# Split weights placed 64 bytes off, or level with, the other operand of their matmuls

## Chip, cores and metric

The kernel runs on one core of one Trainium2 chip. The metric is the device time of one execution in microseconds; the median of three runs of the kernel before is 2693.97 us. All engine names are those of the profile: PE (TensorE), PEld (its weight loads), DVE, ACT, POOL, SP.

## What is computed

The reference runs a two-layer network on one sequence of 512 tokens with a width of 1024, and a further layer behind it, all in float32. Cut to what matters:

```
for layer in range(2):
    h = h + 0.5 * rms_norm(swiglu(rms_norm(h, g[0]), ffn_w_in, ffn_w_out), g[1])
    u = rms_norm(h, g[2])
    m = rwkv7_time_mix(u, ...) if layer == 0 else swa_sinks(u, k_sh, v_sh, ...)
    h = h + rms_norm(m, g[3])
    h = h + 0.5 * rms_norm(swiglu(rms_norm(h, g[4]), ffn_w_in, ffn_w_out), g[5])
x = second_block(h, ...)   # adaptive norm, w_in, two attentions, two branches, w_out, final norm
```

Most of the work is dense products: four feed-forward blocks (1024 to 2 x 2816 and back to 1024), the r, k, v and output projections of the time mix, the projections of the attention, and those of the second block.

## The kernel before

**Products.** A float32 weight is used as two float32r numbers, a high and a low part. `weights` (L146) loads 128 x 1024 weights (512 KB) with a DMA on SP into `wr`, writes the high half of a tile `whl` [128, 2, 1024] on ACT (L153) and the low half on DVE (L154). `mmhl` (L161) issues three products for each 128 x 128 block, L164, L165 and L166: high x high, high x low, low x high. Each has a weight load of its own, and the weight load of the next product runs beside the current product. The moving operand has 512 columns (the whole sequence) or 256 (a half of it). Halves are used where the second half of the sequence is not ready yet, or where the first half has to be done early.

**Feed-forward blocks 0, 2 and 3** (`ffn`, L313; the right-hand pools `a`, `sg`, `wx` are opened there). For hidden columns f = 0, 1, 2 the two halves of the sequence are multiplied one after the other with 256 columns (`gu<-xn`, weights of f = 2 in the pool `wx`). For the other f the products have 512 columns. The way back (`dtile`, L383, tile `o<-a`) comes in two parts: fh = 0 with 512 columns for all 8 output blocks d; fh = 1 with 512 columns for d = 0 and 1, and with 256 columns, first half then second half, for d = 2 to 7. `piece(i)` (L378) makes the weight tiles of that part: 11 pieces of 8 blocks, block b = 11 d + i; pieces 7 to 10 of fh = 1 lie in `wx`.

**Feed-forward block 1** (class `Halves`, L411) works with 256 columns throughout. `xA` (first half) lies in the pool `xnp`, `xB` (second half) in `xb`. `hidden` (L417) takes xA alone for f = 0 to 13, xB alone for f = 11 to 13 and 0 to 10, and both in turn for f = 14 to 21. Its hidden values lie in `xnp` (named `pair`), in `mp` or in the block's own right-hand pool (both named `a`); `out` (L436) multiplies them.

**Time mix** (`dense`, L571; `run`, L813). The first half's `r` projection uses mixed inputs `mx` with float32r weights; the other products of this stage are plain float32 (`mxe` with `wraw`, L592). The chunked recurrence (`Core`) runs beside the second half's projections. `out_half` (L963) is the output projection, with `y` in `xnp` for the first half and in `yb` for the second.

**Attention and second block.** `attention` (L1294) projects q (`psq`), k (`psk`, from `kvn`) and v (`psv`) and multiplies by the output weights (`o<-ohl`). `second` (L1614) multiplies by `w_in2` (`ps<-xn`, `psg<-xn`), by `w_uq` and `w_ukv` (`cqh`, `ckvh`), by the branch weights (`ps<-br`) and by `w_out2` (`o<-mg`). Every third tile of the gates' weights lies in the pool `wsx`, the others in `whl`.

**Memory.** Pools are stacks. One grows from the low addresses of a partition (`left`), the other down from byte 229344 (`right`). Tiles start at multiples of 32 bytes. In the program of before, the start addresses of the operands of these products, modulo 128, are:

```
left   xnp 32   hp 32   mp 32   whl 32   wraw 32   mx 32
right  a 96   wx 96   xb 96   yb 96   lat (cqh, ckvh) 96   lcst (wq) 96   wsx 96   fin (br) 96
right  ato (kvn, ohl) 0
```

The offsets inside the tiles (a block of 512 bytes, the low half 4096 bytes on, a half of the sequence 1024 bytes on) are multiples of 128, so a pool has one remainder. `const` (8096 bytes at byte 1152) lies under the whole left stack. A new tile whose place was held by an older one waits for the last use of that one.

**Order of work.** The instructions of an engine run in the order in which the program gives them; SP issues its transfers in order. Waits come from the tiles alone.

Of the kernel before, what the change touches and what calls it, by code (L numbers as in the profile page):

```python
# [8 lines left out]
F32 = mybir.dt.float32  # L9
# [8 lines left out]
P = 128  # L18
# [2 lines left out]
FT = 22  # L21
FH = 11
HALVES = ((0, 256), (256, 256))
FULL = ((0, 512),)


# [59 lines left out]
class Net:  # L86
    def __init__(self, tc, ctx, ins, outs):
        self.tc, self.nc, self.ctx = tc, tc.nc, ctx
        self.ins, self.outs = ins, outs
        nc = tc.nc  # L90
        self.const = self.pool("const", 1)
        self.tail = iter(())
        self.dead = None
        self.open_x()
        self.open_mm()
        self.ones = self.const.tile([P, P], F32, name="ones")
        nc.vector.memset(self.ones, 1.0)
        self.ident = self.const.tile([P, P], F32, name="ident")
        nc.gpsimd.affine_select(out=self.ident, in_=self.ones, pattern=[[1, P]], compare_op=ALU.is_equal, fill=0.0, base=0, channel_multiplier=-1)
        nv = ins["vecs"].shape[1]  # L100
        self.vecs = self.const.tile([P, nv], F32, name="vecs")
        nc.scalar.dma_start(out=self.vecs, in_=ins["vecs"])
        self.eps = self.const.tile([P, 1], F32, name="eps")
        nc.vector.memset(self.eps, 1e-6)
        self.bk = self.const.tile([P, 2], F32, name="bk")
        nc.scalar.dma_start(out=self.bk, in_=ins["b_k"])
        self.rows = self.const.tile([P, 272], F32, name="rows")
        nc.scalar.dma_start(out=self.rows, in_=ins["rows"])

        self.rx = self.const.tile([P, T], F32, name="rx")  # L110
        self.halfg = self.const.tile([P, 96], F32, name="halfg")
        nc.vector.tensor_scalar(out=self.halfg, in0=self.vecs[:, 0:96], scalar1=0.5, scalar2=None, op0=ALU.mult)
# [30 lines left out]
            self.small = self.pool("small", 2, self.wctx)  # L143


    def weights(self, src, pool=None, cols=1024, hl=None):  # L146

        nc = self.nc
        if hl is None:
            hl = (pool or self.whl).tile([P, 2, 1024], F32R, tag="whl", name="whl")  # L150
        raw = self.wraw.tile([P, 1024], F32, tag="wraw", name="wr")
        nc.sync.dma_start(out=raw[:, :cols], in_=src)
        nc.scalar.activation(out=hl[:, 0, :cols], in_=raw[:, :cols], func=AF.Copy)  # L153
        nc.vector.tensor_tensor(out=hl[:, 1, :cols], in0=raw[:, :cols], in1=hl[:, 0, :cols].bitcast(F32), op=ALU.subtract)  # L154
        return hl
# [157 lines left out]
    def ffn(self, idx, gpost, after_half, side=(), early=()):  # L313
        nc = self.nc
        win, wout = self.ins["ffn_w_in"][idx], self.ins["ffn_w_out"][idx]
        with ExitStack() as es:
            ap = self.pool("a", 12, es, side="right")
            tp = self.sg = self.pool("sg", 2, es, side="right")
            wx = self.pool("wx", 4, es, side="right")
            nsp = 3  # L320
            for fh in range(2):
# [15 lines left out]
                for t0, n in HALVES if first else ():  # L337
                    for f in first:
                        if t0 == 0:
                            a[f] = ap.tile([P, 2, T], F32R, tag="a", name="a")  # L340
                            w[f] = [self.weights(win[2 * f + j], wx if f == 2 else None) for j in range(2)] if f or not early else early
                        ps[f] = self.mm.tile([P, 2, n], F32, tag="mm", name="gu")
                        if t0 == 0:
                            for j in range(2):
                                for k in range(KT):
                                    self.mm3(ps[f][:, j], w[f][j], k, self.xn[k], t0, n, k == 0 and j == 0, k == KT - 1, skip_group_check=True)
                            run(islice(self.tail, 4))
                    if t0:
                        for fl in (first[:2], first[2:]):
                            for k in range(KT):  # L350
                                for f in fl:
                                    for j in range(2):
                                        self.mm3(ps[f][:, j], w[f][j], k, self.xn[k], t0, n, k == 0 and j == 0, k == KT - 1, skip_group_check=True)
                    else:
                        run(self.tail)
                    for f in first:
                        act(f, ps[f][:, 0], ps[f][:, 1], t0, n)
# [19 lines left out]

                def piece(i):  # L378
                    if i not in pcs:
                        pcs[i] = self.weights(wout[fh * 11 + i], wx if fh == 1 and i >= 7 else None)  # L380
                    return pcs[i]

                def dtile(d, t0, n):  # L383
# [27 lines left out]
class Halves:  # L411
# [5 lines left out]
    def hidden(self, f, halves, w=None):  # L417

        N, nc = self.N, self.N.nc
        w = w or [N.weights(self.win[2 * f + j]) for j in range(2)]  # L420
        ps = [N.mm.tile([P, 2, 256], F32, tag="mm", name="gu") for _ in halves]
        for j in range(2):
            for k in range(KT):
                for (x, a, hf), p in zip(halves, ps):
                    N.mm3(p[:, j], w[j], k, x[k], 0, 256, j == 0 and k == 0, k == KT - 1, skip_group_check=True)
                yield
        for (x, a, hf), p in zip(halves, ps):
            r = N.rx[:, 256 * hf:256 * hf + 256]
            s = N.small.tile([P, 2, 256], F32, tag="gu", name="gu", bufs=1)
            nc.vector.tensor_tensor(out=s, in0=p, in1=r[:, None, :].to_broadcast([P, 2, 256]), op=ALU.mult)  # L430
            nc.scalar.activation(out=s[:, 0], in_=s[:, 0], func=AF.Silu)
            nc.vector.tensor_tensor(out=s[:, 0], in0=s[:, 0], in1=s[:, 1], op=ALU.mult)
            nc.scalar.activation(out=a[0], in_=s[:, 0], func=AF.Copy)
            nc.vector.tensor_tensor(out=a[1], in0=s[:, 0], in1=a[0].bitcast(F32), op=ALU.subtract)

    def out(self, fh, halves):  # L436

        N = self.N
        for d in range(KT):
            ps = N.mm.tile([P, 2, 256], F32, tag="mm", name="o")  # L440
            for i in range(FH):
                b = d * FH + i
                if b % 8 == 0:
                    w = N.weights(self.wout[fh * FH + b // 8])
                for j, (a, _) in enumerate(halves):
                    hi, lo = a[fh * FH + i]
                    N.mmhl(ps[:, j], w, b % 8, hi, lo, i == 0 and j == 0, i == FH - 1, skip_group_check=True)
                yield
            for j, (_, sink) in enumerate(halves):
                sink(d, ps[:, j])  # L450
# [62 lines left out]
class Rwkv:  # L513
# [57 lines left out]
    def dense(self, hf, tmp, exact, mx, mxe):  # L571
# [10 lines left out]

        def weights(src, ex):
            if not ex:
                return N.weights(src)
            w = N.wraw.tile([P, 1024], F32, tag="wraw", name="wraw")
            nc.sync.dma_start(out=w, in_=src)
            return w
# [224 lines left out]
    def run(self, h_spill, gpost, gpre, ffn, gffn, after_half):  # L813
# [9 lines left out]
        e1 = ExitStack()  # L823
        tmp = N.pool("tmp1", 1, e1)
        with ExitStack() as e2:
            mx, mxe = N.pool("mx", 12, e2), N.pool("mxe", 16, e2)
            first = self.dense(0, tmp, (0,), (12, lambda: mx.tile([P, 2, 256], F32R, tag="mx", name="mx")), (16, lambda: mxe.tile([P, 256], F32, tag="mxe", name="mxe")))

            run(islice(first, 8))
# [133 lines left out]
    def out_half(self, hf, y, m, h_spill, gpost, after):  # L963
# [3 lines left out]
        nc.sync.dma_start(out=N.h[:, :, t0:t0 + n], in_=h_spill.rearrange("(k p) t -> p k t", p=P)[:, :, t0:t0 + n])  # L967
        acc = N.small.tile([P, n], F32, tag="acc", name="acc")
        for d in range(KT):
            w = N.weights(N.ins["w_rkvo"][3, d])  # L970
            ps = N.mm.tile([P, T], F32, tag="mm", name="o")
            for k in range(KT):
                N.mm3(ps[:, :n], w, k, y[k], 0, n, k == 0, k == KT - 1)
# [320 lines left out]
def attention(N, kvd, rd, gpost, after_half):  # L1294

    nc = N.nc
    W = 128
    with ExitStack() as es:
        one = N.pool("at1", 1, es, side="right")
        qp = N.pool("atq", 2, es, side="right")  # L1300

        oh = N.pool("ato", 8, es, side="right")
        with ExitStack() as e2:
            N.mm, N.st, scp = Turns(N.ma), None, Turns(N.mb, N.mb, N.ms, N.mb, N.ms)
            vec = lambda n: N.vecs[:, 8 * VEC[n]:8 * VEC[n] + 8]
# [20 lines left out]

            early = []
            for t in range(2):
                w = N.weights(N.ins["w_qo"][0, t])
                early.append((w, N.mm.tile([P, T], F32, tag="mm", name="psq")))  # L1330
                for k in range(KT):
                    N.mm3(early[t][1][:, 0:256], w, k, N.xn[k], 0, 256, k == 0, k == KT - 1, skip_group_check=True)
# [2 lines left out]
            for a in range(2):  # L1335
# [2 lines left out]
                for k in range(KT):  # L1338
                    N.mm3(pk[a], w, k, kvn[k], 0, T, k == 0, k == KT - 1)
                run(islice(N.tail, 3))  # L1340
            w = [N.weights(N.ins["w_kv"][2 + j]) for j in range(2)]
            pv = [scp.tile([P, 2, 256], F32, tag="sc", name="psv") for _ in range(2)]
            for k in range(KT):
                j, q = k // 4, slice(256 * (k % 4), 256 * (k % 4) + 256)
# [116 lines left out]
            def out(d, ks, pool=None, t0=0, n=T):  # L1461

                if d not in wo:
                    wo[d] = N.weights(N.ins["w_qo"][1, d])
                if ks[0] == 0:
                    po_[d] = pool.tile([P, T], F32, tag="sc" if pool is scp else "mm", name="o")
                for k in ks:
# [146 lines left out]
def second(N, out, angd, hs):  # L1614
# [61 lines left out]
    with ExitStack() as e1:  # L1676
# [2 lines left out]

        early = []  # L1680
        for i in range(5):
            w, ps = N.weights(N.ins["w_in2"][i]), N.mm.tile([P, T], F32, tag="mm", name="ps")
            for k in range(KT):
                N.mm3(ps[:, 0:256], w, k, N.xn[k], 0, 256, k == 0, k == KT - 1, skip_group_check=True)
            early.append((w, ps))
# [302 lines left out]

    def dtile(d, t0, n):
        if d not in ws:  # L1990
            ws[d] = N.weights(N.ins["w_out2"][d])
        ps = N.mm.tile([P, T], F32, tag="mm", name="o")
        for k in range(KT):
            N.mm3(ps[:, :n], ws[d], k, mg[k], t0, n, k == 0, k == KT - 1)
# [19 lines left out]
def net(tc, ins, out):  # L2014
    with ExitStack() as ctx:
# [8 lines left out]
        N.open_w()  # L2024
        early = []
        for hf in range(2):
            early.append(N.weights(ins["ffn_w_in"][0, hf]))
            N.load_h(ins["xT"], hf)

        def to_products(gcol):  # L2030
# [46 lines left out]
```

## Time and profile before

| | |
|---|---|
| median of 3 runs | 2693.97 us (2688.26 to 2700.58) |
| profiled execution | 2691.58 us |
| its span on the core | 2689.8 us |
| PE, PEld busy | 2613.0 us (97%), 2269.7 us (84%) |
| DVE, ACT, POOL busy | 1477.3 (55%), 1189.4 (44%), 110.5 (4%) |
| mean granted TensorE clock | 0.987 of full speed |
| DMA over the span | 344.21 MB, mean 128 GB/s |

The sum of the prediction is made against the profiled execution; the difference between its time and its span (1.8 us) is what lies around the span. A busy PE is not a PE at its peak: a product is shown with the time that it takes from end to end, and products overlap. The pace of a stream is the distance from one start to the next.

### The profile page before, as it was taken

The page shows a single profiled execution, that of the slowest core. Times are in us where ns is not written, and L with a number is a line of the kernel's source. Part 1 is how long each engine was busy: PE and PEld are TensorE (multiplying, and loading weights), DVE is VectorE, ACT ScalarE, POOL GpSimd, SP SyncE. Part 2 cuts the span into 40 slices and gives each one's busy share as a digit, 9 for nine tenths or more (in the row PEclk, how much of TensorE's full clock was granted, in tenths as well). Part 3 has the DMA queues.
Part 4 walks back from the last instruction along what each step waited for, and adds up shares of the span by engine and source line. Part 5 has one row for each costly group of instructions (what it writes and reads, how often), then busy time and mean ns, then how long its engine had stood idle before and what let it go on. Part 6 is the DMA issues. An engine that isn't in the chain of part 4 may idle for free.

```text
span 2689.8 us, 44078 instructions
## 1 busy us (share of the span) xinstructions
PE 2613.0 (97%) x17458; PEld 2269.7 (84%) x17458; DVE 1477.3 (55%) x3065; ACT 1189.4 (44%) x2156; POOL 110.5 (4%) x140
## 2 busy tenths in 40 slices
PE   8999998899999999999999999999999999999998
PEld 7888897778789999999988889779888898877777
DVE  7734456565647556448652446647424456334655
ACT  5232337555455555345532334556322334445643
POOL 0000000000000000000000000330000000000310
PEclk9999999999999999999999999999999999999999
DMA  6632316774675464235443233112322333213352
GB/s 208 210 111 97 103 62 213 228 205 133 195 226 152 126 214 131 95 111 186 129 148 99 94 118 122 64 40 88 102 94 95 102 103 118 83 45 92 121 166 91
DMA packets 207557, 344.21 MB, mean 128 GB/s; under 512 B 66164, under 2 KB 136180, under 8 KB 207352
## 3 DMA queue, kind: packets, MB, share of 16 engines
q1 hardware_dynamic: 206920, 341.13, 40.1%
q8 instruction: 137, 2.24, 0.3%
q14 instruction: 68, 0.56, 0.1%
q10 hardware_dynamic: 432, 0.28, 0.0%
HBM read 298.51 MB, written 41.26 MB: 126 GB/s over the span
## 4 chain that ended last, share of the span: by engine, by line
PE 86%; DMA 5%; DVE 4%; ACT 2%; issue 1%; SPq 0%; DVEq 0%; ACTq 0%
PE gu L165 11%; PE gu L164 11%; PE gu L166 11%; PE o L164 8%; PE o L166 8%; PE o L165 7%; PE ps L592 3%; PE ps L164 2%; PE ps L165 2%; PE ps L166 2%; PE psg L164 2%; PE psg L165 2%; PE psg L166 2%; PE z L1788 1%; PE st L175 1%
## 5 line engine op out<-in xcount | busy, mean ns | idle before, releaser
L153 ACT ACTIVATE whl<-wr 128x1024 fp32r<-128x1024 f32 x417 | 438.8, 1058 | 722.2 <-PE gu L166 391.8
L154 DVE TENSOR_TENSOR whl<-wr,whl 128x1024 fp32r<-128x1024 f32 x417 | 508.9, 1225 | 378.2 <-ACT whl L153 377.1
L164 PE MATMUL gu<-xn,whl 128*128 128x512 f32 (+1 forms) x1200 | 435.5, 365 | 9.0 <-ACT xn L242 6.9
L165 PE MATMUL gu<-xn,whl 128*128 128x512 f32 (+1 forms) x1200 | 437.7, 366 | 2.2 <-DVE xn L243 2.0
L166 PE MATMUL gu<-xn,whl 128*128 128x512 f32 (+1 forms) x1200 | 436.7, 365 | 0.8 <-DVE whl L154 0.8
L166 PE MATMUL o<-a,whl 128*128 128x256 f32 (+1 forms) x950 | 302.8, 320 | 0.0
L165 PE MATMUL o<-a,whl 128*128 128x256 f32 (+1 forms) x950 | 302.7, 320 | 0.0
L164 PE MATMUL o<-a,whl 128*128 128x256 f32 (+1 forms) x950 | 301.5, 320 | 0.0
L164 PEld LDWEIGHTS gu<-xn,whl 128*128 128x128 f32 x1200 | 226.1, 189 | 45.0 <-ACT xn L242 7.1
L165 PEld LDWEIGHTS gu<-xn,whl 128*128 128x128 f32 x1200 | 226.9, 189 | 39.4 <-DVE xn L243 3.5
L166 PEld LDWEIGHTS gu<-xn,whl 128*128 128x128 f32 x1200 | 227.1, 189 | 37.3 <-DVE whl L154 1.2
L165 PE MATMUL gu<-pair,whl 128*128 128x256 f32 x704 | 199.4, 284 | 1.1 <-DVE pair L243 1.1
L166 PE MATMUL gu<-pair,whl 128*128 128x256 f32 x704 | 198.2, 282 | 1.2 <-DVE whl L154 1.2
L164 PE MATMUL gu<-pair,whl 128*128 128x256 f32 x704 | 198.8, 284 | 0.0
L166 PEld LDWEIGHTS o<-a,whl 128*128 128x128 f32 x950 | 178.9, 188 | 15.4
L165 PEld LDWEIGHTS o<-a,whl 128*128 128x128 f32 x950 | 178.9, 188 | 15.2
L164 PEld LDWEIGHTS o<-a,whl 128*128 128x128 f32 x950 | 178.5, 189 | 15.3
L592 PE MATMUL ps<-mxe,wraw 128*128 128x256 f32 x544 | 135.8, 396 | 6.7 <-DVE mxe L609 3.8
L165 PEld LDWEIGHTS gu<-pair,whl 128*128 128x128 f32 x704 | 133.9, 190 | 2.6 <-DVE pair L243 1.7
L166 PEld LDWEIGHTS gu<-pair,whl 128*128 128x128 f32 x704 | 133.9, 190 | 1.9 <-DVE whl L154 1.4
L164 PEld LDWEIGHTS gu<-pair,whl 128*128 128x128 f32 x704 | 133.5, 190 | 0.9
L592 PEld LDWEIGHTS ps<-mxe,wraw 128*128 128x128 f32 x544 | 103.4, 197 | 27.7 <-issue 6.8
(437 smaller groups left out, 4764.2 us busy)
## 6 DMA issues: line engine op xcount, KB each, us to landing
wr<-in_ffn_w_in_dram SPq DMA_DIRECT2D x204, 512.0 KB, 3.5
wr<-in_ffn_w_out_dram SPq DMA_DIRECT2D x99, 512.0 KB, 3.5
wr<-in_w_in_dram SPq DMA_DIRECT2D x38, 512.0 KB, 3.5
wraw<-in_w_rkvo_dram SPq DMA_DIRECT2D x32, 512.0 KB, 4.7
wr<-in_w_rkvo_dram SPq DMA_DIRECT2D x32, 512.0 KB, 4.6
wr<-in_w_ada_dram SPq DMA_DIRECT2D x24, 512.0 KB, 4.3
wr<-in_w_qo_dram SPq DMA_DIRECT2D x16, 512.0 KB, 3.5
gates<-xf SPq DMA_DIRECT2D x48, 128.0 KB, 1.8
```

The costliest lines, as they stand in the source:

```text
L153: nc.scalar.activation(out=hl[:, 0, :cols], in_=raw[:, :cols], func=AF.Copy)
L154: nc.vector.tensor_tensor(out=hl[:, 1, :cols], in0=raw[:, :cols], in1=hl[:, 0, :cols].bitcast(F32), op=ALU.subtract)
L164: nc.tensor.matmul(ps, lhsT=wh, rhs=xh, start=start, stop=False, **k)
L165: nc.tensor.matmul(ps, lhsT=wh, rhs=xl, start=False, stop=False, **k)
L166: nc.tensor.matmul(ps, lhsT=wl, rhs=xh, start=False, stop=stop, **k)
L175: self.nc.tensor.matmul(ps[:, 256 + c:257 + c], lhsT=sq[:, c * P:(c + 1) * P], rhs=self.ones[:, 0:1], start=first and c == 0, stop=last, s ...
L592: nc.tensor.matmul(ps, lhsT=w[:, b * P:(b + 1) * P], rhs=x, start=start, stop=stop)
L1788: nc.tensor.matmul(seg(z, i, j), lhsT=ntri if j == i else none, rhs=seg(hl[:, x], j), start=False, stop=x == 1 and j == 3, skip_group_chec ...
```

## The change

It adds a tile of 64 bytes to `const`, one of 64 bytes to the right stack in front of `wx`, makes each tile of the pool `whl` 128 bytes longer, (`PAD` is 16 float32 numbers) and lets a caller of `weights` choose with `s` whether the weights begin at the tile's start or 64 bytes on. It opens `mx` on the right, and the pool `ato` in front of `at1` and `atq`. No instruction of an engine is added or taken away.

```diff
@@ Net.__init__
+        self.const.tile([P, PAD], F32, name="pad")
@@ Net.weights
-    def weights(self, src, pool=None, cols=1024, hl=None):
+    def weights(self, src, pool=None, cols=1024, hl=None, s=0):
         if hl is None:
-            hl = (pool or self.whl).tile([P, 2, 1024], F32R, tag="whl", name="whl")
+            if pool:
+                hl = pool.tile([P, 2, 1024], F32R, tag="whl", name="whl")
+            else:
+                hl = self.whl.tile([P, 2080], F32R, tag="whl", name="whl")
+                hl = hl[:, 16 * s:16 * s + 2048].rearrange("p (x c) -> p x c", x=2)
@@ Net.ffn
+            self.pool("wxpad", 1, es, side="right").tile([P, 16], F32, name="wxpad")
             wx = self.pool("wx", 4, es, side="right")
...
-  w[f] = [self.weights(win[2 * f + j], wx if f == 2 else None) for j in range(2)] if f or not early else early
+  w[f] = [self.weights(win[2 * f + j], wx if f == 2 else None, s=1) for j in range(2)] if f or not early else early
...
-  pcs[i] = self.weights(wout[fh * 11 + i], wx if fh == 1 and i >= 7 else None)
+  pcs[i] = self.weights(wout[fh * 11 + i], wx if fh == 1 and i >= 7 else None, s=int(fh == 1 and i >= 2))
@@ Halves.hidden, Halves.out, dense's weights, out_half, and the early weights of net
-  N.weights(...)
+  N.weights(..., s=1)
@@ Rwkv.run
-            mx, mxe = N.pool("mx", 12, e2), N.pool("mxe", 16, e2)
+            mx, mxe = N.pool("mx", 12, e2, side="right"), N.pool("mxe", 16, e2)
@@ attention
+        oh = N.pool("ato", 8, es, side="right")
         one = N.pool("at1", 1, es, side="right")
         qp = N.pool("atq", 2, es, side="right")
-
-        oh = N.pool("ato", 8, es, side="right")
...
+                w = N.weights(N.ins["w_qo"][0, t], s=1)
+            w = [N.weights(N.ins["w_kv"][2 + j], s=1) for j in range(2)]
+                    wo[d] = N.weights(N.ins["w_qo"][1, d], s=int(d >= 3))
@@ second
+            w, ps = N.weights(N.ins["w_in2"][i], s=1), N.mm.tile([P, T], F32, tag="mm", name="ps")
+            ws[d] = N.weights(N.ins["w_out2"][d], s=int(d >= 4))
```

## Rows read from the trace of the kernel before

**Rows 1.** The page: engines over the span, and the chain that ended last, by engine.

```profile
PE 2613.0 (97%) x17458; PEld 2269.7 (84%) x17458; DVE 1477.3 (55%) x3065; ACT 1189.4 (44%) x2156; POOL 110.5 (4%) x140
...
PE 86%; DMA 5%; DVE 4%; ACT 2%; issue 1%; SPq 0%; DVEq 0%; ACTq 0%
```

**Rows 2.** Nine stretches: length, PE, PEld, DVE, ACT, POOL busy, PEclk, DMA share, GB/s.

```profile
0.00:40.00 40.00, 29.50 (x221) 28.02 (x221) 30.97 (x83) 27.52 (x52) 0.78 (x6) 1.00 0.68 217
40.00:385.00 345.00, 343.74 (x1756) 292.94 (x1757) 175.22 (x287) 102.39 (x147) 0.00 (x0) 1.00 0.39 127
385.00:835.00 450.00, 418.76 (x3889) 354.35 (x3889) 278.09 (x767) 250.34 (x563) 23.79 (x40) 0.96 0.66 192
835.00:975.00 140.00, 138.68 (x1483) 132.28 (x1482) 84.85 (x176) 74.50 (x138) 0.88 (x2) 0.98 0.49 151
975.00:1030.00 55.00, 50.78 (x411) 49.18 (x410) 40.57 (x68) 34.48 (x60) 0.00 (x0) 1.00 0.56 182
1030.00:1650.00 620.00, 619.84 (x4133) 568.44 (x4132) 331.99 (x564) 245.40 (x379) 0.00 (x0) 1.00 0.37 120
1650.00:1855.00 205.00, 198.22 (x1429) 167.58 (x1427) 128.19 (x409) 113.17 (x294) 47.52 (x58) 0.98 0.23 79
1855.00:2205.00 350.00, 349.96 (x1806) 298.99 (x1807) 159.76 (x234) 115.70 (x169) 0.00 (x0) 1.00 0.30 100
2205.00:2689.80 484.80, 463.54 (x2344) 377.90 (x2343) 247.69 (x480) 225.84 (x357) 37.55 (x35) 0.98 0.31 101
```

**Rows 3.** Timeline of PE, 256 columns, fh = 1, pieces 2 to 6: 35 rows.

```profile
1631.03 0.28 PE L165 MATMUL o<-a,whl 128*128 128x256 f32 x1
...
1634.88 0.28 PE L166 MATMUL o<-a,whl 128*128 128x256 f32 x1
```

**Rows 4.** Timeline of PE, the same products, pieces 7 to 10: 92 rows.

```profile
1639.10 0.28 PE L166 MATMUL o<-a,whl 128*128 128x256 f32 x1
...
1650.02 0.28 PE L164 MATMUL o<-a,whl 128*128 128x256 f32 x1
```

**Rows 5.** Timeline of PE, 256 columns, block 0, f = 2, second half: 48 rows.

```profile
45.11 0.28 PE L166 MATMUL gu<-xn,whl 128*128 128x256 f32 x1
...
50.44 0.28 PE L165 MATMUL gu<-xn,whl 128*128 128x256 f32 x1
```

**Rows 6.** Timeline of PE, 512 columns, gu from xn: 46 rows.

```profile
99.69 0.39 PE L165 MATMUL gu<-xn,whl 128*128 128x512 f32 x1
...
109.89 0.39 PE L165 MATMUL gu<-xn,whl 128*128 128x512 f32 x1
```

**Rows 7.** Timeline of PE, 512 columns, fh = 0, o from a: 45 rows.

```profile
164.67 0.40 PE L166 MATMUL o<-a,whl 128*128 128x512 f32 x1
...
174.94 0.40 PE L165 MATMUL o<-a,whl 128*128 128x512 f32 x1
```

**Rows 8.** Groups of PE's products by form (line 164 alone; 165 and 166 have equal counts).

```profile
L164 PE MATMUL gu<-xn,whl 128*128 128x512 f32 x912 | 355.1, 389 | 0.0
...
L164 PE MATMUL gu<-pair,whl 128*128 128x256 f32 x704 | 198.8, 284 | 0.0
```

**Rows 9.** Timeline of PE, 256 columns, out_half of the second half: 20 rows.

```profile
984.75 0.28 PE L165 MATMUL o<-pair,whl 128*128 128x256 f32 x1
...
986.99 0.28 PE L166 MATMUL o<-pair,whl 128*128 128x256 f32 x1
```

**Rows 10.** Timeline around 391 us: the first mixes on ACT, and PE's next product.

```profile
390.25 3.69 ACT L608 ACTIVATE mxe<-u,ommu 128x256 f32<-128x256 f32 x9
...
395.07 5.28 PE L592 MATMUL ps<-mxe,wraw 128*128 128x256 f32 x12 [3.81 <-DVE mxe L609]
```

**Rows 11.** Timeline of SP around 1650 us: the loads of kvn.

```profile
1650.57 4.00 SPq L1311 DMA_DIRECT2D kvn<-kvd  x8
```

**Rows 12.** Timeline of PE, 512 columns, cqh with the weights wq: 6 rows.

```profile
2517.14 0.39 PE L164 MATMUL ps<-cqh,wq 128*128 128x512 f32 x1
...
2518.28 0.39 PE L166 MATMUL ps<-cqh,wq 128*128 128x512 f32 x1
```

More of the change, by code (lines that the diff above doesn't have):

```diff
@@ L23 @@
 HALVES = ((0, 256), (256, 256))
+PAD = 16
 FULL = ((0, 512),)
@@ L419, in hidden @@
         N, nc = self.N, self.N.nc
-        w = w or [N.weights(self.win[2 * f + j]) for j in range(2)]
+        w = w or [N.weights(self.win[2 * f + j], s=1) for j in range(2)]
         ps = [N.mm.tile([P, 2, 256], F32, tag="mm", name="gu") for _ in halves]
@@ L443, in out @@
                 if b % 8 == 0:
-                    w = N.weights(self.wout[fh * FH + b // 8])
+                    w = N.weights(self.wout[fh * FH + b // 8], s=1)
                 for j, (a, _) in enumerate(halves):
@@ L584, in weights @@
             if not ex:
-                return N.weights(src)
+                return N.weights(src, s=1)
             w = N.wraw.tile([P, 1024], F32, tag="wraw", name="wraw")
@@ L969, in out_half @@
         for d in range(KT):
-            w = N.weights(N.ins["w_rkvo"][3, d])
+            w = N.weights(N.ins["w_rkvo"][3, d], s=1)
             ps = N.mm.tile([P, T], F32, tag="mm", name="o")
@@ L1328, in attention @@
             for t in range(2):
-                w = N.weights(N.ins["w_qo"][0, t])
+                w = N.weights(N.ins["w_qo"][0, t], s=1)
                 early.append((w, N.mm.tile([P, T], F32, tag="mm", name="psq")))
@@ L1340, in attention @@
                 run(islice(N.tail, 3))
-            w = [N.weights(N.ins["w_kv"][2 + j]) for j in range(2)]
+            w = [N.weights(N.ins["w_kv"][2 + j], s=1) for j in range(2)]
             pv = [scp.tile([P, 2, 256], F32, tag="sc", name="psv") for _ in range(2)]
@@ L1463, in out @@
                 if d not in wo:
-                    wo[d] = N.weights(N.ins["w_qo"][1, d])
+                    wo[d] = N.weights(N.ins["w_qo"][1, d], s=int(d >= 3))
                 if ks[0] == 0:
@@ L1681, in second @@
         for i in range(5):
-            w, ps = N.weights(N.ins["w_in2"][i]), N.mm.tile([P, T], F32, tag="mm", name="ps")
+            w, ps = N.weights(N.ins["w_in2"][i], s=1), N.mm.tile([P, T], F32, tag="mm", name="ps")
             for k in range(KT):
@@ L1990, in dtile @@
         if d not in ws:
-            ws[d] = N.weights(N.ins["w_out2"][d])
+            ws[d] = N.weights(N.ins["w_out2"][d], s=int(d >= 4))
         ps = N.mm.tile([P, T], F32, tag="mm", name="o")
@@ L2026, in net @@
         for hf in range(2):
-            early.append(N.weights(ins["ffn_w_in"][0, hf]))
+            early.append(N.weights(ins["ffn_w_in"][0, hf], s=1))
             N.load_h(ins["xT"], hf)
```

## The prediction

> **What bounds the kernel now.** First the page's engines and the chain of waits [rows 1]: PE is busy 97% of the span and holds 86% of the chain that ended last; DVE, the next engine, holds 4%. Then the stretches [rows 2]: four of them (40 to 385, 835 to 975, 1030 to 1650, 1855 to 2205 us) leave PE idle at most 1.3 us each. They are 1455 us of 2689.8. Idle stands elsewhere: 10.5, 31.2, 4.2, 6.8 and 21.3 us in the other five. PE is not short of clock: it was granted 0.96 to 1.00 of the 2.4 GHz level in every stretch. So the time is what the streams of products take, and what they take is their pace, the distance between starts.
>
> The timeline gives the pace. The same line of code, `o<-a` in the way back of feed-forward block 2, runs 35 products in 3.85 us, 34 steps of 113.2 ns [rows 3], and a few microseconds later, with nothing between starts that PE waited for, 92 products in 10.92 us, 120.0 ns a step [rows 4]. Form, moving tiles and engines beside it are the same. What differs is where the weights lie: pieces 2 to 6 in `whl` (remainder 32 modulo 128, moving operand `a` 96: 64 off), pieces 7 to 10 in `wx` (96 and 96: alike). It is not the pool by itself: where `wx` weights meet xn at 32, 64 off, 48 products take 5.33 us, 113.4 ns a step [rows 5]. With 512 columns it is the other way round: 226.7 ns for `gu<-xn`, 32 and 32 (10.20 us over 45 steps) [rows 6], and 233.4 ns for `o<-a`, 32 and 96 (10.27 us over 44 steps) [rows 7]. The profile holds no addresses; the pairing with them is mine, from the pools' remainders.
>
> **The change, part by part.**
>
> *Remainders.* The pad lengthens `const` by 64 bytes, and the whole left stack goes from 32 to 96: `xnp`, `mp`, `whl`. A `whl` tile of 8320 bytes is 65 x 128, so all five begin at 96, and with s = 1 the weights begin at 32. `wxpad` takes `wx` to 32. The `ato` pool, now first on the right stack, goes from 0 to 96 (229344 minus 8 x 4096), and `mx`, first on the right too, to 96. So nearly every moving operand stands at 96, and s alone decides.
>
> *256 columns, from alike to 64 off.* Counted by code in blocks of three products: `gu<-pair` with xA 352 of the 704 [rows 8] (22 f x 16), `o<-a` 216 (3 x 64 from `wx`, 24 from `mp`), `gu<-xn` 192, `o<-pair` 192, `mx` 128, `ps<-xn` 80, `o<-mg` 64, `psq` 32: 1256 blocks, 3768 products. The price of one lies between 120.0 - 113.2 = 6.8 ns [rows 3, 4] and 120.0 - 117.9 = 2.1 ns, since one stream that is 64 off already, `yb`, runs at 117.9 (2.24 us over 19 steps) [rows 9]. I take 6.0: nearer to the first, which comes from most of such products, with something off for streams in which short groups alternate.
>
> *512 columns, from 64 off to alike.* `o<-a` 312 blocks (3 x 88 in fh = 0, 3 x 16 with pieces 0 and 1; piece 2 stays off), `br` 64, gates out of `wsx` 32, `cqh`, `ckvh` and the second `psv` 32: 440 blocks, 1320 products at 233.4 - 226.7 = 6.7 ns [rows 6, 7]; I take 6.6. The 912 blocks of `gu<-xn` [rows 8] are alike before and after: nothing.
>
> *32 off, to the right kind.* With `kvn` and `ohl` now at 0, 336 products of 256 columns and 120 of 512 are 32 off. The trace has no long run of them; between nothing and 6.8 ns, I take half: 3.3 ns, 1.5 us in all.
>
> *Where it counts.* By the stretches of [rows 2], in starts of the trace (256 | 512), at 6.0 and 6.6 ns:
>
> 0 to 40: 163 | 0, 1.0 us
> 40 to 385: 174 | 312, 3.1 us
> 385 to 835: 630 | 0, 3.8 us
> 835 to 975: 779 | 0, 4.7 us
> 975 to 1030: 150 | 0, 0.9 us
> 1030 to 1650: 957 | 312, 7.8 us
> 1650 to 1855: 197 | 0, and the 32-off ones, 2.7 us
> 1855 to 2205: 270 | 312, 3.7 us
> 2205 to the end: 448 | 384, 5.2 us
>
> Sum 32.9 us. In the four stretches without idle, 19.3 us, I count all: nothing there arrives later than PE asks for it. In the others, 13.6 us, PE waits for ACT, DVE or a DMA again and again; where what it waits for does not hang on PE itself, the gain only lengthens the wait. I count half, 6.8 us: the ends are nothing and all, and no row says which waits hang on PE.
>
> *The moved pools.* `mxe` slides down onto the last `wx` tile, which is read to the last product of block 0, while `mx` comes to lie on `a`. Before, the first mixes began at 390.25 us, some 0.8 us ahead of the end of that product, and PE then waited 3.81 us for them [rows 10]. The first can now begin only behind it: 0.8 us lost. `kvn` moves onto `a` tiles; before, its loads began at 1650.57 [rows 11], at the end of the last product of block 2, held by the last `wx` tile, and the `a` tile under its first place is read until one block earlier: nothing. The pads, the longer tiles and the offset put no work on any engine: ACT and DVE write as many elements as before, and no queue gets a transfer more or an order of its own.
>
> Gain 19.3 + 6.8 - 0.8 = 25.3 us: the profiled execution of 2691.58 us becomes 2666.3. That execution is 2.4 us under the median of the three runs, 2693.97; for the median I say 2668.7 us.
>
> **What the skill says against it.** The trace has the two paces side by side. The Trainium skill (SBUF — State Buffer, section "Who interferes with whom") gives PE two independent read ports, one for the moving operand and one for weight loads, and says that PE never waits on anyone. By that rule the address of one operand relative to the other is worth nothing, and the time would stay at 2694; the paces of [rows 3, 4] speak against it, and rival A carries its chance. The page says nothing of remainders modulo 128.
>
> **The rivals.**
>
> *A. Nothing moves* (2694 us). The paces differ for a reason that only goes along with the pool, such as the bytes' height in the partition, and the shift by 64 changes nothing. For: the profile shows no addresses, and `yb`, 64 off, is at 117.9. Against: `wx` weights are fast with xn and slow with `a` [rows 4, 5], and `whl` weights fast with `a` [rows 3]; height alone does not sort these three. Chance 0.04.
>
> *B. Slower* (2698 us). With 512 columns it is not the difference that decides but whether either operand stands at 96: the fast streams of the trace stand at 32 and 32, the slow ones have a 96 in them. After the change all stand at 96 and 96. Then 912 blocks of `gu<-xn` [rows 8], 160 of `psg`, 72 of `ps`, 48 of `psq`, 32 of `o<-mg` and 32 of `psv`, 3768 products, lose 6.6 ns each: 18.1 us with `gu<-xn`, in stretches without idle, and half of 6.8 us elsewhere, 21.5 us, and the 1320 gain nothing. Of the 256-column gain 13.1 us stay in the stretches without idle (2180 products) and half of 9.5 elsewhere, 17.8 us. Net about 4 us slower. The corner of 96 and 96 with 512 columns is rare before: six products with the weights `wq`, 228 ns on average over 5 steps [rows 12], nearer to 226.7 than to 233.4. With 256 columns three of the four corners are in [rows 3 to 5], and the difference sorts them. Chance 0.05.
>
> *C. Feeding sets the pace* (2679 us). 24 products of 113.2 ns use up 512 KB of weights in 2.72 us, 193 GB/s; the stretches in which 256 columns prevail already moved 182 to 217 GB/s [rows 2]. If DMA, ACT or DVE can give no more there, the idle of PE grows by what the products save, and only the stretches 40 to 385, 1030 to 1650 and 1855 to 2205 pay: 14.6 us. Against: 217 GB/s has been moved, with 0.68 of the DMA engines busy. Chance 0.11.
>
> **The numbers.** The forecast has 0.80. Its own ends: 2.1 ns for 256 columns and the four stretches alone give 4.6 + 6.2 = 10.8 us, 2683; 6.8 and 6.7 ns everywhere give 36.5 us, 2657. The range 2657 to 2683 takes in C; A and B lie outside. About 0.5%, 13.5 us, is what a measurement of this kernel can tell from no change. Faster by more: the forecast but its upper end, and most of C, 0.84. Within: A, most of B and the rest of those, 0.14. Slower: what is left of B, 0.02.
>
> **What would show it.** In the profile after: `o<-a` with pieces 7 to 10 and `gu<-pair` with xA near 114 ns a step, `o<-a` of fh = 0 near 227, `gu<-xn` with 512 columns still 226.7. The stretches without idle should be shorter by 3.1, 4.7, 7.8 and 3.7 us, and the idle in the others larger by some 7 us together. If `gu<-xn` goes to 233, B is right; if the paces stay, A; if the paces fall and the four stretches do not shrink, C. Wrong in size if the products reach their pace and the idle takes more than half, or nothing, of the other five stretches.

## The result and the profile after

The changed kernel took 2709.32 us (median of 6, 2704.83 to 2711.35) against 2694.84 us for the kernel before in the same job (6 runs, 2688.26 to 2700.58): ratio 1.0055, 95% interval 1.004 to 1.0069. It is slower by half a per cent; the forecast was 25 us faster.

The page of the changed kernel (profiled execution 2704.83 us), its busy time and the first line of its chain of waits; they answer to [rows 1]:

```profile
span 2703.1 us, 44081 instructions
PE 2622.4 (97%) x17458; PEld 2275.4 (84%) x17458; DVE 1476.8 (55%) x3065; ACT 1188.8 (44%) x2156; POOL 110.6 (4%) x140
PE 86%; DMA 6%; DVE 4%; ACT 3%; issue 1%; SPq 0%; DVEq 0%; ACTq 0%
```

As many instructions but for three (44078 before), the same work on DVE and ACT, and still a PE that is busy 97% of the time and holds 86% of the chain. So the time came from the pace of PE's products, its waits or its clock. All three moved.

**Paces.** PE's timeline, two weight tiles of `gu<-xn` with 512 columns, one after the other (start, duration, line, operands):

```profile
60.29 0.39 PE L172 MATMUL gu<-xn,whl 128*128 128x512 f32 x1
...
65.96 0.39 PE L173 MATMUL gu<-xn,whl 128*128 128x512 f32 x1
66.18 0.40 PE L174 MATMUL gu<-xn,whl 128*128 128x512 f32 x1
...
71.77 0.40 PE L174 MATMUL gu<-xn,whl 128*128 128x512 f32 x1
```

25 steps in 5.67 us, 226.8 ns, and then 24 steps in 5.59 us, 232.9 ns. Before, they ran at 226.7 [rows 6]. The tiles take turns like this through the kernel: two of the pool's five places are slow, and 1126 of the 2728 steps measured of `gu<-xn` are at 232.6 ns. And `o<-a` with 256 columns at the end of block 2, nearly all of it the pieces in `wx`, once for the first half of the sequence and once for the second:

```profile
1615.33 0.28 PE L172 MATMUL o<-a,whl 128*128 128x256 f32 x1
...
1626.44 0.28 PE L174 MATMUL o<-a,whl 128*128 128x256 f32 x1
...
1638.83 0.28 PE L174 MATMUL o<-a,whl 128*128 128x256 f32 x1
...
1650.13 0.28 PE L174 MATMUL o<-a,whl 128*128 128x256 f32 x1
```

98 steps in 11.11 us, 113.4 ns, as forecast; then 96 steps in 11.30 us, 117.7 ns, although all are 64 or 192 bytes off. Two paces, each held for a whole stream.

**Waits and clock.** Aligning the traces by the same products (the n-th of a name) shows where the 13.3 us between the two spans arise. At the first `psg` product (2327.5 us before) the changed kernel is 1.3 us behind, after swinging by several us either way in the recurrence; from there to the 300th it needs 148.0 us instead of 136.2. That is 11.8 us in one place, the second block's attention, where `psg` products fill the time in which DVE prepares `hl` for the products `z`. PE's waits in it, longest groups first (us in total, times, longest):

```profile
PE z L1797 <- DVE hl L1789: 5.7, 3, 4.4
PE z L1797 <- DVE hl L1790: 1.6, 1, 1.6
PE z L1775 <- ACT e L1798: 1.3, 1, 1.3
PE ps L172 <- ACT oa L1806: 0.7, 1, 0.7
PE pv L1805 <- ACT e L1798: 0.3, 1, 0.3
```

and the changed kernel's stretches there (start:end, length, then busy time of PE, PEld, DVE, ACT, POOL with counts, granted clock, DMA share, GB/s):

```profile
2343.00:2350.00 7.00, 4.92 (x27) 3.85 (x26) 6.96 (x8) 4.96 (x5) 0.00 (x0) 1.00 0.49 154
2350.00:2364.00 14.00, 13.17 (x36) 8.73 (x35) 4.66 (x6) 1.24 (x1) 0.00 (x0) 0.51 0.23 76
2364.00:2412.00 48.00, 46.66 (x224) 35.30 (x223) 13.77 (x17) 20.16 (x19) 0.00 (x0) 1.00 0.14 47
```

In 7 us around 2346 PE idles for 2.1 us, waiting twice for DVE; then its clock is granted at 0.51, close to the 1.2 GHz level, for 14 us in which it executes 36 products. Had the clock been full there, about seven of those 14 us would have been saved: an estimate, 14 x (1 - 0.51). The kernel before has waits of 4.4 and 0.4 us behind `hl` in the whole stretch and a granted clock of 0.97:

```profile
PE z L1788 <- DVE hl L1780: 4.4, 1, 4.4
PE z L1788 <- DVE hl L1781: 0.4, 1, 0.4
PE pv L1796 <- ACT e L1789: 0.3, 1, 0.3
2327.50:2463.70 136.20, 131.02 (x618) 102.07 (x618) 53.28 (x64) 67.09 (x62) 0.29 (x1) 0.97 0.23 73
```

**The cause of the waits** stands in the order of PE's instructions, which was to stay. From the first `psg` product on, the starts of the trace give, in runs of products (`z`: those that read `hl`, in groups of 10):

```
before   psg 58, z 10, psg 1, z 10, psg 13, z 20
after    psg 72, z 30
```

In the kernel before the gates' products stand between the groups of `z`; in the changed one they all come first, and three groups of `z` meet a DVE that has not finished `hl`. The source gives both in the same order; the framework that schedules the program arranges the instructions by a simulated timeline, so the order on an engine is not that of the source. The second run below shows that longer tiles alone bring the new order; by which steps they do was not traced.

### The profile page after: what moved, and what is told of

It reads as the page before. It is cut to its first block, busy times and chain, and to the rows that moved or that the text cites. A ratio compares the mean times of both kernels' runs of the same rounds, so it can differ in the third digit from the quotient of the medians.

```text
span 2703.1 us, 44081 instructions
## 1 busy us (share of the span) xinstructions
PE 2622.4 (97%) x17458; PEld 2275.4 (84%) x17458; DVE 1476.8 (55%) x3065; ACT 1188.8 (44%) x2156; POOL 110.6 (4%) x140
## 4 chain that ended last, share of the span: by engine, by line
PE 86%; DMA 6%; DVE 4%; ACT 3%; issue 1%; SPq 0%; DVEq 0%; ACTq 0%
PE gu L173 12%; PE gu L172 12%; PE gu L174 12%; PE o L172 7%; PE o L174 7%; PE o L173 7%; PE ps L601 4%; PE ps L172 2%; PE ps L174 2%; PE ps L173 2%; PE psg L172 1%; PE psg L173 1%; PE psg L174 1%; DMA wr<-in_ffn_w_in_dram 1%; PE z L1797 1%
## 5 line engine op out<-in xcount | busy, mean ns | idle before, releaser
L172 PEld LDWEIGHTS gu<-xn,whl 128*128 128x128 f32 x1200 | 226.8, 190 | 47.7 <-ACT xn L250 7.7
L338 DVE TENSOR_TENSOR av<-gu,rx 128x512 f32<-128x512 f32 (+1 forms) x75 | 46.9, 625 | 150.3 <-PE gu L174 150.3
```

The source lines that it names most:

```text
L172: nc.tensor.matmul(ps, lhsT=wh, rhs=xh, start=start, stop=False, **k)
L338: nc.vector.tensor_tensor(out=av, in0=u, in1=r, op=ALU.mult)
```

## The experiments

Two theories. **M**: with 512 columns the difference between the start of the weights and that of the moving operand decides modulo 256, and the changed tiles, 8320 bytes apart (an odd multiple of 128), alternate between level (a difference of 0) and 128 off. **O**: the second block's 12 us come from the changed order.

**1. Streams by themselves.** One tile of weights, two moving tiles, nothing else running; `stream` issues the three products of `mmhl` 32 times.

```diff
+for r in range(2):
+    for n in (256, 512):
+        for m, ds in ((0, range(0, 256, 32)), (96, range(0, 256, 64))):
+            for d in ds if r == 0 else reversed(ds):
+                ps = stream(f"c{n}m{m}d{d}r{r}", n, m, d, 4)
```

> Nothing of the network is computed: 96 products with 256 or with 512 columns for each distance between the start of the weights and the start of the moving operand (0 to 224 bytes in steps of 32, moving operand at remainder 0; 0, 64, 128 and 192 with it at 96), all from one tile of weights, each stream once in each direction. Theory M (the distance modulo 256 decides): 512 columns 227 ns a step at 0, 232.7 at 128, 233 at 64, 230 at 192, 233 at 32; 256 columns 119 to 120 at 0 and at 128, and 113.3 or 117.8 at 64 and at 192. Rival K (the prediction's rule, modulo 128): 512 columns 227 at 128 as well. Rival N (the address decides nothing, the slow tiles have another cause, such as the place of the tile in the pool): all distances alike within 1 ns. In M and K, 96 for the moving operand changes nothing against 0.

PE's timeline, first and last product of some streams (the name tells columns, remainder of the moving operand and distance):

```profile
165.82 0.39 PE L38 MATMUL c512m0d0r<-X,W 128*128 128x512 f32 x1
...
187.36 0.40 PE L40 MATMUL c512m0d0r<-X,W 128*128 128x512 f32 x1
...
254.87 0.39 PE L38 MATMUL c512m0d128r<-X,W 128*128 128x512 f32 x1
...
276.94 0.40 PE L40 MATMUL c512m0d128r<-X,W 128*128 128x512 f32 x1
...
443.64 0.28 PE L38 MATMUL c256m0d192r<-X,W 128*128 128x256 f32 x1
...
454.41 0.28 PE L40 MATMUL c256m0d192r<-X,W 128*128 128x256 f32 x1
```

95 steps each: 226.7, 232.3 and 113.4 ns. All streams:

```
distance      512 columns       256 columns
0             226.7             120.0
32            233.3             118.3
64            233.4             117.8 (3 streams), 113.5 (1)
96            234.2             117.3
128           232.3 to 233.3    118.6 to 120.0
160           233.4             119.9
192           228.9             117.8 (3 streams), 113.3 (1)
224           233.3             116.6 and 117.8
```

With 512 columns 128 costs 5.6 to 6.6 ns a product where the prediction's rule has 0: M holds, K and N fall. The moving operand at 96 gives the same numbers. With 256 columns one and the same distance can have two paces.

**2 to 4. One part at a time.**

```diff
# second: before, longer tiles alone
-hl = (pool or self.whl).tile([P, 2, 1024], ...)
+hl = self.whl.tile([P, 2080], ...)[:, 0:2048]
# third: change, short tiles in the second block, weights at their start
-N.open_w(hl=4)
+N.open_w(hl=4, wl=2048)
...
# fourth: change, five one-tile pools of 8256 and 8384 bytes, and 128 bytes ahead of the right stack;
# i is the number of the pool, from a fixed list SLOTS
...
+o = 48 * (1 - s) if i % 2 else 16 * s
+hl = self.whl[i].tile([P, 2096 if i % 2 else 2064], ...)[:, o:o + 2048]
```

> The kernel before with only the longer weight tiles (8320 bytes, all weights at the tile's start). Theory M (512 columns: distance modulo 256): gu<-xn with 512 columns alternates by weight tile between 227 and 232.7 ns, 2736 / 2 x 5.8 ns = 7.9 us lost; o<-a of fh = 0 stays slow. Theory O (the second block loses some 12 us from 2327 to 2477 us because longer tiles change what overlaps what, and with it the order in which the instructions of that stage are given): 12 us lost there. Both: 2713 us; M alone: 2702; O alone: 2706; neither (the prediction's modulo 128, and the loss comes from the pads, the offsets or the clock): 2694.

> The changed kernel, but in the second block the weight tiles are 8192 bytes again, all weights at the tile's start; the order of the products from 2300 to 2480 us is then that of the kernel before. Theory O: the 12 us of that stretch are given back, 2697 us; its stalls z behind DVE are as before (one of some 4.4 us in place of three of 5.7) and its granted clock has one dip in place of four. Rival Q (the stretch is long because of paces or clock that the rest of the change brings): 2707 to 2710, since the psg products all at 227 give back only 1.6 us, and ps and o<-mg with 256 columns lose 2.

> The changed kernel with every weight tile placed so that the weights begin, modulo 256, level with the moving operand for 512 columns (5181 of 5245 steps, in place of 2750 of 5181) and 64 bytes off for 256 columns (5786 steps at 64, 939 at 192), whatever place of the pool the tile has; the order of PE is that of the changed kernel but for some 60 instructions near 2250 to 2390 us. Theory M: gu<-xn, o<-a and psg with 512 columns all near 227 ns, 2268 x 5.5 ns = 12.5 us given back: 2697 us. If the place of the second block's loss (theory O) falls away by chance with the 60 instructions, 2686. Rival K (modulo 128): 2709 as the change.

The kernel before took 2697.61 us here (19 runs). The second kernel: 2721.02 us, ratio 1.0082 (1.0059 to 1.0106). The longer tiles alone, which move no weight relative to 128, cost by the medians more than the whole change: the steps of `gu<-xn` with 512 columns are at 227.2 ns (1610 of them, level) and at 232.7 (1123, 128 off), and the stretch in the second block is 13.5 us longer, with the order of the changed kernel (`psg` 72 in a row). Both theories together had priced it at 19 us; it is 23.

The third: 2695.1 us, ratio 0.999 (0.9972 to 1.0007), where the change had 1.0055. 12 us were to come back; by the ratios it is 17. The stretch gives back 11.5 of them, with the waits and the clock of before:

```profile
PE z L1799 <- DVE hl L1791: 4.4, 1, 4.4
2330.10:2466.60 136.50, 131.47 (x618) 102.27 (x618) 53.31 (x65) 67.15 (x62) 0.29 (x1) 0.97 0.23 72
```

O is shown, and it holds over all profiles of this case: the stretch from the first to the 300th `psg` takes 135.0 to 136.4 us in the five with the order of before, 148.0 to 149.7 in the three with that of the change, and 149.4 to 154.1 in the four with a third order that the fourth run brought. The fourth: 2693.09 us, ratio 0.9988 (0.9968 to 1.0007), with all tiles of `gu<-xn` at one pace, here four in a row, 96 steps of 226.7 ns:

```profile
59.83 0.39 PE L180 MATMUL gu<-xn,whl 128*128 128x512 f32 x1
...
81.59 0.39 PE L180 MATMUL gu<-xn,whl 128*128 128x512 f32 x1
```

M is shown in the kernel too. Its second block has that third order (`psg` 22, other products `z`, `psg` 50, then the groups of `z`) and still loses 9 us: the 300th `psg` is 149.4 us behind the first, 13.2 more than before, but the first no longer comes behind those other `z`, which took 4.1 us ahead of it.

**5 to 7. Both repairs; the recurrence; the price of 256 columns.**

```diff
# fifth: fourth with short tiles in the second block
+N.open_w(hl=4, turns=False)
# sixth: fifth with
-mx = N.pool("mx", 12, e2, side="right")
+mx = N.pool("mx", 12, e2)
# seventh: fifth, all weights level
-o = 48 * (1 - s) if i % 2 else 16 * s
+o = 48 if i % 2 else 0
-self.pool("wxpad", 1, es, side="right").tile([P, 16], F32, name="wxpad")
```

> The weight tiles of the fourth experiment (level with the moving operand modulo 256 for 512 columns, 64 off for 256) and, in the second block, the tiles of the third (8192 bytes, weights at the start). Theories M and O together: the two repairs add, 2709 - 12.5 - 13.5 = 2683 us, and by the fourth run less the stretch at 2327 to 2464, 2693 - 13 = 2680. Rival (the two runs were lucky in the same place, and one loss stays): 2690 to 2695.

> The fifth kernel with the pool mx on the left again: the order of the products from 400 to 950 us is that of the kernel before. Its 384 products then are 128 off in place of 64, at most 2 us lost. Theory S (the moved pool and the changed order of the recurrence cost the 5 to 7 us that the traces lose from 391 to 835 us): 5 us faster than the fifth, 2677. Rival (that stretch differs from one execution to the next by as much, since the kernel with the longer tiles alone lost 6.8 us there with the order of before): within 3 us of the fifth, or 1 to 2 us slower.

> The fifth kernel with the 256-column products level with their moving operand as well (6815 steps at 0, none at 64); the order of the instructions is that of the fifth. So the price of 64 bytes for 256 columns by itself. By the two paces of the traces (113.3 and 117.8, on average 116.4 in the fourth run, against 119.2 to 120): 3.2 ns x 6536 steps = 21 us if all of it were on the path, 12 to 16 us with the cover of the stretches in which PE waits: 2692 to 2696. By the prediction's 6.0 ns: 39 us, 25 to 32 on the path: 2705 to 2712. If it is worth nothing: 2680.

Measured against 2690.88 us (22 runs): 2690.77 (ratio 1.0, 0.9985 to 1.0015), 2699.87 (1.0038, 1.0024 to 1.0052) and 2709.15 (1.0071, 1.0053 to 1.009). The fifth is a miss, and its trace says why: the second block has the order of the fourth run (`psg` 22 and 50) and loses the same 9 us. With the pool split into five the short tiles do not bring the old order back, so only one of the two repairs was in it. The sixth speaks against theory S: the order of before from 400 to 950 us is no better. It is 9 us slower than the fifth, more than its rival allowed too; about half of that stands in the second block, where its stretch takes 154.1 us against 149.5. The seventh differs from the fifth in the distance of 256-column weights alone:

```profile
339.77 0.28 PE L180 MATMUL o<-a,whl 128*128 128x256 f32 x1
...
361.97 0.28 PE L179 MATMUL o<-a,whl 128*128 128x256 f32 x1
```

185 steps in 22.20 us, 120.0 ns. Over all such steps 118.92 ns against 115.67: 3.25 ns x 6580 = 21 us, of which 18 us are found in the median. The offset by 64 bytes is worth what the two paces say on average, about half of the 6.0 ns I had put in; and more of it reaches the time than the 12 to 16 us expected.

**8. What sets 113 or 118?**

```diff
+stream("a256", 256, 0, 8 + i); stream("after256", 256, 64, 16)
+stream("a512", 512, 0, 8 + i); stream("after512", 256, 64, 16)
+nc.scalar.activation(out=Y[:, 0, :256], in_=ps[:, :256], func=AF.Copy); stream("afterwait", 256, 64, 16, Y)
```

> Nothing of the network is computed: 36 streams of 48 products with 256 columns, 64 bytes off, 12 of them behind products of 256 columns at 0, 12 behind products of 512 columns at 0, 12 behind a wait of PE for ACT. Theory F (the pace of such a stream is set as it starts and then held): within a stream the steps keep to 113.3 or to 117.8 on average, and both occur among the 12 starts of a kind. Rival D (what goes before decides): each kind of start gives one pace. Rival E (other engines decide, since in the kernel DVE, ACT and the DMAs are busy beside PE): with all other engines idle one pace only, 113.3.

All 24 streams behind other products: 117.8 from the first step to the last. Of the 12 behind a wait, 11 settle at 113.3 within a dozen steps, one stays at 117.8. One of the 11:

```profile
395.80 0.39 PE L40 MATMUL afterwait<-Y,W 128*128 128x256 f32 x1 [0.53 <-ACT Y L53]
...
396.83 0.28 PE L42 MATMUL afterwait<-Y,W 128*128 128x256 f32 x1
...
401.25 0.28 PE L42 MATMUL afterwait<-Y,W 128*128 128x256 f32 x1
```

From the ninth product on these are 39 steps in 4.42 us, 113.3 ns. D is nearest: the kind of start goes with the pace, but for one of 36, and other engines are not needed for the slow one. But the third kind also has another moving tile, and in the changed kernel the `o<-a` stream shown above, in the same pieces, goes from 113.4 to 117.7 at 1630 us, where nothing but four products `st` with one column stands between, and no wait. Which start gives which pace stays open. It differs between executions too: of all stretches of 12 steps at 64 or 192, 80% keep the fast pace in one profile of the kernel before and 90% in the other, 47% in both of the changed kernel, 29% in the fourth run.

**9 and 10. Both repairs without splitting the pool.** One pool again; the weights are put into a tile by the place that it has (`SLOTS`, the sequence of places).

```diff
# ninth: third with
-s = 16 * s if self.wl > 2048 else 0
+i = int(SLOTS[self.turn])
+self.turn += 1
+s = 0 if self.wl == 2048 else 16 if s == 1 else 32 * ((i + s // 2) % 2)
...
-pcs[i] = self.weights(..., s=int(fh == 1 and i >= 2))
+pcs[i] = self.weights(..., s=1 if fh == 1 and i >= 2 else 2)
... # and s=2 or s=1 at two calls in attention
# tenth: ninth with mx on the left
```

> The third kernel (second block with tiles of 8192 bytes, its order from 2300 to 2480 us that of the kernel before) in which the weights of 512-column products are put 0 or 128 bytes into the tile by the place of the tile, so that they begin level modulo 256 with xn, a, kvn or ohl; 4766 steps at 0, 416 at 128 (gates, latents and branches of the second block). 256 columns stay 64 or 192 off. Theories M, O together: the third run's 2695 less the pace of 512 columns (229.84 to 227.3 over some 5200 steps, 13 us) is 2682; the fifth run's 2691 less the 9 us that it lost at 2301 to 2464 is 2682 as well. Rival (the losses come in other places whenever products are shortened): 2690 or more.

> The ninth kernel with mx on the left: its order of products is that of the kernel before but for some 50 instructions from 1800 to 1870 and near 2250 us. If the order that the moved pool gives from 400 to 950 us is the better one, as the sixth run against the fifth says (9 us), 2691. If that difference belonged to the sixth kernel's order in the second block (18 us lost there against 13), the two are alike but for 1.5 us of mx at 128: 2684.

Against 2690.21 us (23 runs): 2677.61 us, ratio 0.996 (0.9944 to 0.9976), and 2680.82 us, ratio 0.9966 (0.9949 to 0.9983). Both beat the kernel before and, by the ratios, the change. In the ninth the order is `psg` 58, `z` 10, 1, 10, 13, 20 again, and the stretch in the second block, first to 300th `psg`, is shorter than before:

```profile
2309.30:2444.50 135.20, 130.21 (x617) 100.94 (x616) 53.25 (x64) 67.08 (x62) 0.29 (x1) 0.99 0.22 73
```

From the change's 1.0055 to 0.996 are 26 us. The traces account for about 25: the stretch is 13 us shorter, and the 512-column steps together take 12 us less.
The place of `mx` makes no difference that this can tell.

**11 and 12. How much belongs to one execution.** Both kernels unchanged.

> The kernel before, unchanged, for a second profile: how much of the time at half clock belongs to the program, and how much to one execution. Theory H (the order of a program sets its waits and so its stretches at half clock): no stretch at half clock from 2330 to 2400 us, one of 6.8 us from about 2407, and 30 to 38 us lost to half clock in all. Rival (chance): stretches at other places, and a loss that may be anything from 30 to 50.

> The changed kernel, unchanged, for a second profile. Theory H: again some 13.7 us at half clock from about 2350 us, behind two or three waits within 10 us, and 46 to 56 us lost to half clock in all. Rival (chance): none there, and a loss from 30 to 50.

One execution each: 2696.18 us and 2696.22 us, equal, and the second is 9 us below the lowest of the changed kernel's six executions above. Span and granted clock, before and changed:

```profile
core 0: 2694.5 us, clock 0.982
```

```profile
core 0: 2694.5 us, clock 0.985
```

Half a miss. The second block does as theory H says: 148.0 us again in the changed kernel, 14 us at half clock behind the same two waits, and none of that in the kernel before. But the total at half clock changes from one execution to the next. Taken as the time lost to it (half of the time at half clock), it is 36 and 49 us in two profiles of the kernel before, and 50 and 42 in two of the changed one. Of the 13 us between the two of before, 8.5 sit between 390 and 1060 us, in the recurrence, where short products alternate with waits; in the changed kernel no one place holds most of the difference. So two single profiles can't be compared to better than some 10 us, and the medians of many runs must. They say that the clock is part of the change's loss: its six executions were granted 0.979 to 0.981 of the clock, some 54 us lost, and the 19 of the kernel before that stand beside experiments 2 to 4 were granted 0.984 in the median, some 43 lost. About 7 of these 11 us have a place, the second block; the others have none that the runs show.

## Why the prediction was wrong

Profile against profile, after less before. The paces are means over all steps at full clock between two products of that kind, 5115 with 512 columns and 6580 with 256; the forecast stands at its full price, ahead of what waits were to swallow, and without its 1.5 us for products 32 off. Half clock is the time lost to it:

```
                          forecast        trace
512 columns               -8.7 us         228.83 to 230.02 ns, +6.1 us
256 columns               -22.6           116.45 to 114.77 ns, -11.1
half clock                 0              35.6 to 50.2 us lost, +14.6
rest (waits, moved pools)  +0.8           +3.7
sum                                       +13.3
```

The rest is what PE's idle grew by, from 2689.8 - 2613.0 = 76.8 us to 2703.1 - 2622.4 = 80.7. Of the 14.6 us, 6.8 stand in the stretch of the second block; the others are within what two executions of one program differ by. Four steps of the prediction failed: the remainder modulo 128, the price for 256 columns, the order that was to stay, and the clock, which had no term.

- **"A `whl` tile of 8320 bytes is 65x128, so all five begin at 96"**: true modulo 128, and that was the step that turned the sign of a whole term, for modulo 256 they alternate. Of the 512-column products the change was to speed up, `o<-a` got 2.7 of the 6.6 ns (233.3 to 230.6), and two in five of the 2736 of `gu<-xn`, costed at nothing, lost 5.8 ns each. The trace of before couldn't show it: its tiles lie 8192 bytes apart, so no product of 512 columns stood at a distance of 128. I read a rule with two values where the rows [rows 6, 7] only tell 0 from 64. Rival B had the right products slower for another reason (an operand at 96); the first run, with the moving operand at 96 and the weights level, shows 226.7, so B's mechanism falls.
- **6.0 ns for 256 columns.** The direction was right; the size was 3.6: products that were alike went, within their streams, from 119.2 to 115.6 (forecast: 120.0 to 114). The lower bound that I took from `yb`, 117.9 [rows 9], was no outlier, but the second pace of the same distance. And the 2690 steps that were off already went from 114.8 to 115.6, since fewer streams now keep the fast pace (47% of their stretches in place of 80 or 90%): 0.8 x 2690 = 2.2 us given back.
- **"No queue gets ... an order of its own."** None got more work, but PE, DVE, ACT and SP got another order from the scheduler. This is the largest single loss in one place: 11.8 us, of which 4.5 us are waits (9.6 against 5.1 us in the stretch) and about 7 the clock that fell behind them. The third run gives it back by one tile size.
- **"PE is not short of clock."** A granted clock of 0.96 to 1.00 in every stretch hid 35.6 us lost, and the sum let that stand unchanged. It rose with the new order, by 6.8 us in the second block alone.
- **32 off.** `o<-ohl` with 256 columns went from 118.3 to 114.7 ns: 3.6 ns, for 3.3 taken. With 512 columns it gained 2.4 ns and `psk` 0.7.
- **The moved pools, 0.8 us.** The first mixes did begin later, at 391.65 us behind block 0's last product, as forecast. But PE waited 1.53 us for them, where it had waited 3.81 [rows 10]: 2.3 us won in place of 0.8 lost. With `mx` on the right it is 1.54 in the ninth run, on the left 3.81 in the tenth; why it is shorter isn't shown. The two runs' medians can't tell so little.
- **Half of the gain for the waits, 6.8 us.** Not needed: PE idled 75.5 and 78.1 us in the ninth and tenth run, with both rules right, against 76.8 before. So rival C falls too: the paces fell, and PE waited no longer than before.
- **Which part of the gain counts.** In the four stretches without idle, the ninth run, which has both rules right, saves 2.7 us in 40 to 385 (forecast 3.1) and 3.0 in 1855 to 2205 (forecast 3.7). In 1030 to 1650 it saves 2 us, and 7.8 was too much: `gu<-pair` before stood at 116.8 on average, with both distances mixed, and after at 115.7, 1.1 ns in place of half of 6.0. Of 835 to 975, at the end of the recurrence, the runs say little: up to the 500th `gu<-pair` the ninth run gains 6.7 us and the tenth loses 1.6 with the same distances, while the two profiles of the kernel before differ there by 4.4.
- **Rival A** falls: distance alone moves 2709 to 2691 us in the seventh and fifth runs. In the first run, with nothing else running, the distance of the two operands changes a product's pace from 226.7 to 233.4 ns. The Trainium skill (SBUF — State Buffer, section "Who interferes with whom") gives PE two independent read ports and says that PE never waits on anyone. What the prediction took from this, that the distance is worth nothing, does not agree with the run; the measurement decides.

## What to carry to other kernels

When a padding is added to shift operands, work out the address of every buffer of a rotating pool, and modulo twice the period that you believe in. Two rows that differ in one distance say nothing of the distances that the trace doesn't contain; a kernel of bare streams settles them in one run. Where instructions are ordered by a simulated timeline, a change of a tile's size is a change of the order: compare the order of the two programs on each engine before any sum is made.

## What the runs showed of the hardware

In a stream of products the pace depends on where the weights begin relative to the moving operand; whether it is the weights in use or those loaded beside them, no run tells apart. With 512 columns it is 226.7 ns level, 228.9 at 192, 232.3 to 234.2 elsewhere, modulo 256. With 256 columns level is among the slowest, 120.0 ns, as are 128 and 160, and 64 and 192 have two steady paces, 113.3 and 117.8, that are taken within a dozen steps of the stream's start and kept for 90 products and more; behind four short products, without a wait, a stream went from the one to the other, and what decides is open. And two waits within 5 us, 2.1 us of idle together, were followed by 14 us at 0.51 and 0.50 of the clock in the two profiles of the changed kernel: the idle is the smaller part of its price. The price is not set by the length of a wait alone: the single wait of 4.4 us further on went with 6.8 or 6.9 us at half clock in both kernels, and with 3.4 in the ninth run.
